# A hybrid recurrent decoder step: the end in three stretches, the merges and the residual's norm on VectorE, the samples' passes spread

## The chip, the cores and the metric

The kernel runs on one core of one Trainium2 chip. The metric is the device time of one execution in microseconds (us); smaller is better. The engines are TensorE (PE, with its weight loads as PEld), VectorE (DVE), ScalarE (ACT), GpSimd (POOL) and the DMA queues that SyncE (SP) and ScalarE issue.

## The reference

One layer is computed for 544 tokens that share all weights: a prompt of 512 and eight samples of 4 tokens. Model width 1024, feed-forward width 4096, all in float32.

```python
proj = x @ w_in + b_in                    # gates, queries, keys, values of three branches
o, s = _gated_linear_scan(q, k, v, g, s0)     # GLA and HGRN2; mLSTM has a scan of its own
gates = sigmoid(mg).reshape(..., 3, D_MODEL)
merged = (gates[:, :, 0] * (h_gla @ w_up_gla)
          + gates[:, :, 1] * (h_ml @ w_up_ml)
          + gates[:, :, 2] * (h_hg @ w_up_hg))
x = _layernorm(DN_ALPHA * x + merged @ w_out, ln1_g, ln1_b)
hid = square(relu(x @ w_ff_up))
x = _layernorm(DN_ALPHA * x + hid @ w_ff_down, ln2_g, ln2_b)
```

The outputs are x and the branches' new states, for the prompt and for the samples.

## The kernel before

**Layout and precision.** Activations are kept transposed: the channels lie on 128 partitions (KD = 8 column tiles for the width of 1024), and the 544 tokens are the free dimension, in two halves of HT = 272. Each operand of a large product is split into a rounded part (`h`) and the rest (`l`) in the type fp32r, and each product is three matmuls per block of 128: wh·xh, wh·xl, wl·xh. For each of them both halves of the tokens are streamed, each into its half of a PSUM tile of the pool `psg` (two buffers). `mm` (L145) writes these matmuls, and nearly all of TensorE's work is its line L158. `gemm` (L163) gets a weight tile ready by `wload` (L133): SP's queue loads `raw`, ScalarE copies it to `wh` (L141), VectorE subtracts to get `wl` (L142), two buffers each. A 128x1024 weight tile has 48 matmuls.

**Stages, in order of time.** The input projections; the mLSTM branch in chunks of 128 tokens; the GLA branch and the HGRN2 branch (`gated`, names with `hg`), whose matmuls run between those of the projections; the merges; the output projection and the first norm's sums; two feed-forward blocks (`blk`) of 16 up tiles (`wff1`, k = x1h, x1l) and 8 down tiles (`wff2`, k = hidh, hidl); the last norm and the stores of y.

- *Samples' passes* (L503): in `gated`, the state of each of eight samples (`Ss`) is multiplied with 2x4 columns of the queries, for two pairs of heads; 16 matmuls in a group, one group in GLA (96 weight columns), one in HGRN2 (64). A matmul in plain f32 shows as two records in the trace.
- *Merges* (class `Merge`): a tile of gates is multiplied with a product from PSUM (L871, VectorE), and in the second and third branch it is added to `merged` (L875, POOL); in the third, the sum is split to `mh` and `ml`, the operands of the output projection.
- *Up tiles*: the norm isn't applied to x1 ahead of the product. It is folded in behind it: VectorE adds `ne` times a column sum (L1029, this reads PSUM), multiplies by `rstd` (L1030), ScalarE takes relu and square, and the result is split. `ne` and `rstd` come from `ln_sums` (L978: TensorE sums `a1`, `a2` over the partitions with a matrix of ones) and `ln_end` (L985, L988).
- *Residual's norm* (L1042 to L1044): the normed x1 itself is wanted only by the down tiles of the first block. From the third up tile on, one column tile beside each up tile: POOL adds `ne`, POOL multiplies by `rstd`, ScalarE applies scale and bias.
- *The end* (L1069 to L1102): the last two column tiles of the second block (`last`, i = 0 and 1) aren't done in full width one after the other. Their four weight tiles (`lh`, `ll`) stay in SBUF; for the first half of the tokens both column tiles are computed (96 matmuls), then the norm's sums of this half are closed, and its norm, in 8 column tiles (VectorE L1092, L1096; ScalarE L1100) and four stores (L1102), lies beside the matmuls of the second half. What follows the second half's last matmul is the tail of the kernel.

**What sets the order.** Each engine takes its instructions in one fixed order. That order is made by a scheduler that is given the program in the order of the code; it plays the engines forward with costs of its own, and of the instructions that are ready in that play it takes the one of highest priority, by default the earlier in the code. `tc.high_priority(OFF)` lifts an instruction far ahead of that; with a negative argument it is put as many places later. DMA transfers of weights stand in SP's queue in their order.

Of the kernel before, what the change touches and what calls it, by code (L numbers as in the profile page):

```python
# [42 lines left out]
def build(tc, I, O):  # L43
    nc = tc.nc
    with ExitStack() as ctx:
# [83 lines left out]
        def vcol(c):  # L129
            return vec[:, c:c + 1]  # L130
# [11 lines left out]
                nc.vector.tensor_tensor(out=l[:, 0:n], in0=raw[:, 0:n], in1=h[:, 0:n].bitcast(F32), op=ALU.subtract)  # L142
            return h, l

        def mm(ps, units, ah, al, ext=0, halves_=(0, 1), between=None):  # L145


            nk = sum(u[2] for u in units)
            k = 0
            for u, (h, l, n) in enumerate(units):  # L150
                if u and between:
                    between()
                for i in range(n):
                    wh, wl = h[:, i * 128:(i + 1) * 128], l[:, i * 128:(i + 1) * 128]
                    for s, (w, a) in enumerate(((wh, ah), (wh, al), (wl, ah))):
                        for hf in halves_:
                            w_ = HT + (ext if hf else 0)
                            nc.tensor.matmul(  # L158
                                ps[:, hf, 0:w_], w, a(k)[:, hf * HT:hf * HT + w_],
                                start=(k == 0 and s == 0), stop=(k == nk - 1 and s == 2))  # L160
                    k += 1

# [184 lines left out]
        def gated(q, k, b, sc, dv, vtok, sname, nt, gate):  # L347
# [142 lines left out]
            def sample():  # L490
                at, P, qx, k3 = (st[2][n] for n in ("at", "P", "qx", "k3"))
                oT = psr.tile([128, 512], F32, tag="r", name="oTs")
                for h in range(4):
                    nc.tensor.matmul(oT[0:dv, h * 32:(h + 1) * 32], vtok[0:32, 4, h * dv:(h + 1) * dv], at[0:32, h, 0:32],
                                     start=(h == 0), stop=False)
                v3 = stack_v(vtok[0:32, 4, 0:d4], d4)
                nb = 512 // dv // 4 * 4
                yield
                for p in range(2):
                    Ss = t1.tile([128, 8, 97], F32, tag="Ss", name="Ss")  # L500
                    nc.scalar.dma_start(out=Ss[:, :, 0:dv], in_=I[sname][p])
                    for n in range(8):
                        nc.tensor.matmul(  # L503
                            oT[0:dv, p * 64:(p + 1) * 64].rearrange("p (a b) -> p a b", a=2)[:, :, 4 * n:4 * n + 4],
                            Ss[:, n, 0:dv], qx[:, p, n], start=False, stop=(p == 1 and n == 7))
                    yield
                    vxs = [spread_v(v3[:, (2 * p + e) * dv:(2 * p + e + 1) * dv], dv, True) for e in range(2)]
                    for n0 in range(0, 8, nb):
                        kvs = psr.tile([128, 512], F32, tag="r", name="kvs")
                        for e in range(2):  # L510
                            nc.tensor.matmul(kvs[:, 0:nb * dv], k3[:, p, e, :], vxs[e][:, n0 * dv:(n0 + nb) * dv], start=(e == 0), stop=(e == 1))
                        for n in range(n0, n0 + nb):
                            nc.vector.scalar_tensor_tensor(
                                Ss[:, n, 0:dv], Ss[:, n, 0:dv], P[:, p, 4 * n + 3:4 * n + 4],
                                kvs[:, (n - n0) * dv:(n - n0 + 1) * dv], ALU.mult, ALU.add)
                    nc.scalar.dma_start(out=O[sname + "_s"][p], in_=Ss[:, :, 0:dv])
                    yield
# [324 lines left out]
        class Merge:  # L842
# [23 lines left out]
            def products(self, m0, n=4):  # L866
                for m in range(m0, m0 + n):
# [3 lines left out]
                        nc.vector.tensor_tensor(out=halves(merged[:, m, :] if self.first else g), in0=ps, in1=halves(g), op=ALU.mult)  # L871
                    if self.first:
                        continue
                    eng = nc.gpsimd
                    eng.tensor_tensor(out=merged[:, m, :], in0=merged[:, m, :], in1=g, op=ALU.add)  # L875
# [98 lines left out]
        def ln_sums(hf, stop=True):  # L974
            s = slice(hf * HT, (hf + 1) * HT)
            ps = [psr.tile([128, 512], F32, tag="r", name=n) for n in ("m1", "m2")]
            for p, a in zip(ps, (a1, a2)):
                nc.tensor.matmul(p[:, 0:HT], onesn, a[:, s], start=True, stop=stop)  # L978
            return ps

        def ln_end(hf, sums, more=()):
            s = slice(hf * HT, (hf + 1) * HT)
            p1, p2 = sums
            for p, a in zip(sums, more):
                nc.tensor.matmul(p[:, 0:HT], onesn, a, start=False, stop=True)  # L985
            e2 = rstd[:, s]
            nc.scalar.activation(out=e2, in_=p1[:, 0:HT], func=AF.Square)
            nc.vector.tensor_tensor(out=e2, in0=p2[:, 0:HT], in1=e2, op=ALU.subtract)  # L988
            nc.scalar.activation(out=ne[:, s], in_=p1[:, 0:HT], func=AF.Copy, scale=-1.0)
# [22 lines left out]
            nc.vector.scalar_tensor_tensor(halves(x1[:, m, :]), halves(xr), ALPHA, ps, ALU.mult, ALU.add)  # L1012
            ln_tile(x1, m, slice(0, T), put_x1)
        for hf in range(2):
            ln_end(hf, ln_sums(hf))
        mps.close()


# [1 line left out]
        for blk in range(2):  # L1020
            hid = []
            deep = [hl3("hdh", "hh"), hl3("hdl", "hl")] + [w6.tile([128, 3 * T], F32R, tag="w6", name="hdw").rearrange("p (a b) -> p a b", a=3) for i in range(2)]
            for m in range(16):
# [13 lines left out]
                    l = fp.tile([128, T], F32R, tag=f"hidl{m}", name="hidl")  # L1037
                split(h, l, r_)
                hid.append((h, l))
                if blk == 0 and 2 <= m < 2 + KD:  # L1040
                    y = x1[:, m - 2, :]
                    nc.gpsimd.tensor_tensor(out=y, in0=y, in1=ne, op=ALU.add)  # L1042
                    nc.gpsimd.tensor_tensor(out=y, in0=y, in1=rstd, op=ALU.mult)  # L1043
                    nc.scalar.activation(out=y, in_=y, func=AF.Identity, scale=vcol(V_L1G + m - 2), bias=vcol(V_L1B + m - 2))  # L1044
# [21 lines left out]
        for i in range(2):  # L1066
            y = x1[:, KD - 2 + i, :]
            nc.vector.tensor_tensor(out=y, in0=y, in1=cm, op=ALU.subtract)
        pss = [psg.tile([128, 2, 512], F32, tag="g", name="g") for i in range(2)]  # L1069
        def last(i, hf, sl, between=None):  # L1070
            y = x1[:, KD - 2 + i, sl]
            mm(pss[i], units[2 * i:2 * i + 2], hh_, hl_, halves_=(hf,), between=between)
            sq = ftile("sq")
            with tc.high_priority(OFF):
                nc.vector.tensor_tensor(out=y, in0=y, in1=pss[i][:, hf, 0:HT], op=ALU.add)
                nc.scalar.activation(out=sq[:, sl], in_=y, func=AF.Square)
            return y, sq[:, sl]

        for hf in range(2):
            sl = slice(hf * HT, (hf + 1) * HT)  # L1080
            y, sq = last(0, hf, sl)
            with tc.high_priority(OFF):
                nc.vector.tensor_tensor(out=a1[:, sl], in0=a1[:, sl], in1=y, op=ALU.add)
                nc.vector.tensor_tensor(out=a2[:, sl], in0=a2[:, sl], in1=sq, op=ALU.add)
            ends = []
            more = last(1, hf, sl, lambda: ends.append(ln_sums(hf, False)))
            with tc.high_priority(OFF):
                ln_end(hf, ends[0], more)
            for m in range(KD):
                y = x1[:, m, sl]  # L1090
                eng = nc.gpsimd if m in ADDP else nc.vector
                eng.tensor_tensor(out=y, in0=y, in1=ne[:, sl], op=ALU.add)  # L1092
            for m in range(KD):
                y = x1[:, m, sl]
                eng = nc.gpsimd if m in MULP else nc.vector
                eng.tensor_tensor(out=y, in0=y, in1=rstd[:, sl], op=ALU.mult)  # L1096
                if m in AFFD:
                    nc.vector.tensor_scalar(y, y, vcol(V_L2G + m), vcol(V_L2B + m), ALU.mult, ALU.add)
                else:
                    nc.scalar.activation(out=y, in_=y, func=AF.Identity, scale=vcol(V_L2G + m), bias=vcol(V_L2B + m))  # L1100
# [124 lines left out]
```

## Time and profile before

| | us |
|---|---|
| three runs | 940.23, 935.35, 938.45 |
| their median | 938.45 |
| the profiled execution | 940.08 |
| its span in the trace | 938.2 |
| TensorE busy in it | 916.5 (98%) |
| VectorE busy | 556.8 (59%) |
| ScalarE busy | 437.4 (47%) |
| POOL busy | 101.1 (11%) |
| mean granted TensorE clock | 0.991 |

The trace counts from the start of the span. "L158" is line 158 of the kernel before; in the changed kernel lines lie a few further down (L158 is L162 there, L1029 is L1034, L1096 is L1102). A row of a timeline has the start, the time from the first to the last of the instructions that it groups, engine, line and operation, out<-in, the shape, their count, and in brackets the idle time ahead with what ended it. A row of a matmul has the active rows*columns of the weights ahead of the streamed shape. Rows by stretches have busy time (with the number of instructions) of PE, PEld, DVE, ACT and POOL, and then the granted clock (1.00 is full), the share of the DMA engines and the GB/s.

### The profile page before, as it was taken

The page shows a single profiled execution, that of the slowest core. Times are in us where ns is not written, and L with a number is a line of the kernel's source. Part 1 is how long each engine was busy: PE and PEld are TensorE (multiplying, and loading weights), DVE is VectorE, ACT ScalarE, POOL GpSimd, SP SyncE. Part 2 cuts the span into 40 slices and gives each one's busy share as a digit, 9 for nine tenths or more (in the row PEclk, how much of TensorE's full clock was granted, in tenths as well). Part 3 has the DMA queues.
Part 4 walks back from the last instruction along what each step waited for, and adds up shares of the span by engine and source line. Part 5 has one row for each costly group of instructions (what it writes and reads, how often), then busy time and mean ns, then how long its engine had stood idle before and what let it go on. Part 6 is the DMA issues. An engine that isn't in the chain of part 4 may idle for free.

```text
span 938.2 us, 17454 instructions
## 1 busy us (share of the span) xinstructions
PE 916.5 (98%) x7279; PEld 900.4 (96%) x7279; DVE 556.8 (59%) x959; ACT 437.4 (47%) x824; POOL 101.1 (11%) x92
## 2 busy tenths in 40 slices
PE   9999999999999999999999998999999999999995
PEld 7998999999999998999999998999999999999994
DVE  5885568858788577874458656553222355545435
ACT  4296132875636674634444356552111354442315
POOL 0301231001001003131110092000000000000000
PEclk9999999989999999999999999999999999999998
DMA  7311132114132213132234322222222222222302
GB/s 264 121 69 68 59 113 83 40 46 135 41 113 73 76 29 110 35 98 87 68 113 146 106 68 90 92 90 89 86 79 86 90 91 91 91 89 77 105 23 96
DMA packets 37598, 82.73 MB, mean 88 GB/s; under 512 B 12708, under 2 KB 18340, under 8 KB 37520
## 3 DMA queue, kind: packets, MB, share of 16 engines
q1 hardware_dynamic: 25072, 73.28, 24.0%
q10 hardware_dynamic: 12384, 8.33, 3.1%
q8 instruction: 57, 0.93, 0.4%
q14 instruction: 21, 0.17, 0.1%
q0 software_dynamic: 64, 0.02, 0.0%
HBM read 76.51 MB, written 5.09 MB: 87 GB/s over the span
## 4 chain that ended last, share of the span: by engine, by line
PE 86%; DVE 5%; POOL 3%; ACT 3%; DMA 1%; issue 1%; POOLq 0%; ACTq 0%; DVEq 0%
PE g L158 73%; PE lv L406 3%; PE g L83 2%; DVE wl L142 2%; POOL merged L1043 1%; ACT wh L141 1%; POOL merged L1042 1%; DMA Cs<-in_mC 1%; PE o L463 1%; POOL cvo L586 1%; PE oTs L503 1%; PE oTm L763 1%; PE qkp L676 0%; DMA fw<-in_wfirst 0%; PE oT L282 0%
## 5 line engine op out<-in xcount | busy, mean ns | idle before, releaser
L142 DVE TENSOR_TENSOR wl<-raw,wh 128x1024 fp32r<-128x1024 f32 (+2 forms) x139 | 158.1, 1138 | 144.0 <-ACT wh L141 142.2
L141 ACT ACTIVATE wh<-raw 128x1024 fp32r<-128x1024 f32 (+2 forms) x139 | 133.2, 958 | 231.0 <-PE g L158 196.4
L158 PE MATMUL g<-xh,wl 128*128 128x272 f32 x752 | 161.9, 294 | 2.9 <-DVE wl L142 2.9
L158 PE MATMUL g<-xl,wh 128*128 128x272 f32 x752 | 160.3, 292 | 0.0
L158 PE MATMUL g<-xh,wh 128*128 128x272 f32 x752 | 159.8, 292 | 0.0
L158 PEld LDWEIGHTS g<-xh,wl 128*128 128x128 f32 x752 | 120.1, 190 | 5.1 <-DVE wl L142 4.7
L158 PEld LDWEIGHTS g<-xl,wh 128*128 128x128 f32 x752 | 120.0, 190 | 0.8 <-issue 0.5
L158 PEld LDWEIGHTS g<-xh,wh 128*128 128x128 f32 x752 | 119.7, 190 | 0.9 <-issue 0.2
L158 PE MATMUL g<-x1h,wh 128*128 128x272 f32 (+1 forms) x512 | 106.5, 289 | 3.2 <-DVE relu L1029 3.2
L158 PE MATMUL g<-x1l,wh 128*128 128x272 f32 (+1 forms) x512 | 106.7, 289 | 0.0
L158 PE MATMUL g<-x1h,wl 128*128 128x272 f32 (+1 forms) x512 | 106.0, 288 | 0.0
L158 PEld LDWEIGHTS g<-x1h,wh 128*128 128x128 f32 x512 | 80.8, 189 | 3.6 <-DVE relu L1029 3.6
L158 PEld LDWEIGHTS g<-x1l,wh 128*128 128x128 f32 x512 | 81.5, 190 | 0.1
L158 PEld LDWEIGHTS g<-x1h,wl 128*128 128x128 f32 x512 | 81.0, 188 | 0.0
L1031 ACT ACTIVATE relu<-relu,gw 128x544 f32<-128x544 f32 x32 | 24.0, 750 | 77.2 <-DVE relu L1030 77.2
L158 PE MATMUL g<-hidh,wh 128*128 128x272 f32 x280 | 58.1, 288 | 0.0
L158 PE MATMUL g<-hidl,wh 128*128 128x272 f32 x280 | 58.1, 289 | 0.0
L158 PE MATMUL g<-hidh,wl 128*128 128x272 f32 x280 | 57.8, 288 | 0.0
L158 PEld LDWEIGHTS g<-hidl,wh 128*128 128x128 f32 x280 | 44.0, 188 | 0.0
L158 PEld LDWEIGHTS g<-hidh,wl 128*128 128x128 f32 x280 | 43.9, 188 | 0.0
L158 PEld LDWEIGHTS g<-hidh,wh 128*128 128x128 f32 x280 | 43.8, 188 | 0.0
L410 DVE COPY_PREDICATED at<-lmask,lv 128x512 f32<-128x512 int32 (+1 forms) x32 | 26.2, 819 | 22.2 <-PE lv L406 18.2
(399 smaller groups left out, 1695.4 us busy)
## 6 DMA issues: line engine op xcount, KB each, us to landing
raw<-in_wff SPq DMA_DIRECT2D x64, 512.0 KB, 3.5
raw<-in_win SPq DMA_DIRECT2D x47, 512.0 KB, 3.3
xr<-in_xT SPq DMA_DIRECT2D x16, 272.0 KB, 3.3
raw<-in_wout SPq DMA_DIRECT2D x8, 512.0 KB, 3.9
out_yT<-merged SPq DMA_DIRECT2D x8, 272.0 KB, 2.2
fw<-in_wfirst ACTq DMA_DIRECT2D x8, 256.0 KB, 5.2
raw<-in_wup_ml SPq DMA_DIRECT2D x8, 192.0 KB, 2.3
raw<-in_wup_gla SPq DMA_DIRECT2D x8, 192.0 KB, 2.3
```

Of the source, the lines that this page charges most:

```text
L83: nc.tensor.matmul(first_ps[i][hf], w[:, i * 128:(i + 1) * 128], a[:, k, hf * HT:(hf + 1) * HT], start=(k == 0 and n == 0), stop=(k == KD ...
L141: nc.scalar.activation(out=h[:, 0:n], in_=raw[:, 0:n], func=AF.Copy)
L142: nc.vector.tensor_tensor(out=l[:, 0:n], in0=raw[:, 0:n], in1=h[:, 0:n].bitcast(F32), op=ALU.subtract)
L158: nc.tensor.matmul(ps[:, hf, 0:w_], w, a(k)[:, hf * HT:hf * HT + w_], start=(k == 0 and s == 0), stop=(k == nk - 1 and s == 2))
L406: nc.tensor.matmul(lv[0:R, o:o + 2 * H].rearrange("p (a b) -> p a b", a=2), Kv[:, p, c * R:(c + 1) * R], Q[:, p, :, c * H:(c + 1) * H], st ...
L410: nc.vector.copy_predicated(atv.rearrange("p h (n m) -> p h n m", m=2 * m)[:, :, :, m:2 * m], lmask[0:R, li, 0:H].rearrange("p (n m) -> p ...
L463: nc.tensor.matmul(o[:, h * dv:(h + 1) * dv], at[:, c * 4 + h, :], vtok[:, cc, h * dv:(h + 1) * dv], start=(h == 0), stop=(cc == 0 and h = ...
L503: nc.tensor.matmul(oT[0:dv, p * 64:(p + 1) * 64].rearrange("p (a b) -> p a b", a=2)[:, :, 4 * n:4 * n + 4], Ss[:, n, 0:dv], qx[:, p, n], s ...
L586: nc.gpsimd.tensor_copy(cvo[:, :, 0, :], xcp[:, :, 512:515])
L763: nc.tensor.matmul(oT[0:97, h * 32 + 4 * n:h * 32 + 4 * n + 4], Cs[:, n, :], qF[h][:, 4 * n:4 * n + 4], start=False, stop=(h == 3 and n == 7))
L1031: nc.scalar.activation(out=r_, in_=r_, func=AF.Relu, bias=gw[:, 1:2])
L1042: nc.gpsimd.tensor_tensor(out=y, in0=y, in1=ne, op=ALU.add)
```

## The change

1. **The end in three stretches.** `LAST = (0, 272, 408, 544)`: the last two column tiles are finished for 272, then 136, then 136 tokens. `mm_to` takes a list of (output, first token) in place of a choice of halves, and each stretch and column tile takes its own PSUM tile. `ln_sums` and `ln_end` take a slice.
2. **Merges.** The additions to `merged` go from POOL to VectorE: 16 instructions.
3. **The residual's norm.** The additions of `ne` and the multiplications by `rstd` go from POOL to VectorE, 16 instructions; column tile m // 2 gets its addition beside an even up tile m, and its multiplication and ScalarE's pass beside the odd one that follows. It starts with up tile 0 and not 2.
4. **The samples' passes.** Each of the matmuls of L503 gets a priority 380 + 4n places later (`BEHIND`), n being the sample.

The choices of engine `ADDP`, `MULP`, `AFFD`, all empty before, are taken out, which changes nothing.

```diff
+BEHIND = 380
+LAST = (0, 272, 408, 544)
...
-                        for hf in halves_:
-                            w_ = HT + (ext if hf else 0)
+                        for o, t0 in outs:
                             nc.tensor.matmul(
-                                ps[:, hf, 0:w_], w, a(k)[:, hf * HT:hf * HT + w_],
+                                o, w, a(k)[:, t0:t0 + o.shape[-1]],
...
                     for n in range(8):
-                        nc.tensor.matmul(
+                        with tc.high_priority(-(BEHIND + 4 * n)):
+                            nc.tensor.matmul(
...
-                    eng = nc.gpsimd
-                    eng.tensor_tensor(out=merged[:, m, :], in0=merged[:, m, :], in1=g, op=ALU.add)
+                    nc.vector.tensor_tensor(out=merged[:, m, :], in0=merged[:, m, :], in1=g, op=ALU.add)
...
-                if blk == 0 and 2 <= m < 2 + KD:
-                    y = x1[:, m - 2, :]
-                    nc.gpsimd.tensor_tensor(out=y, in0=y, in1=ne, op=ALU.add)
-                    nc.gpsimd.tensor_tensor(out=y, in0=y, in1=rstd, op=ALU.mult)
-                    nc.scalar.activation(out=y, in_=y, func=AF.Identity, scale=vcol(V_L1G + m - 2), bias=vcol(V_L1B + m - 2))
+                if blk == 0:
+                    y = x1[:, m // 2, :]
+                    if m % 2 == 0:
+                        nc.vector.tensor_tensor(out=y, in0=y, in1=ne, op=ALU.add)
+                    else:
+                        nc.vector.tensor_tensor(out=y, in0=y, in1=rstd, op=ALU.mult)
+                        nc.scalar.activation(out=y, in_=y, func=AF.Identity, scale=vcol(V_L1G + m // 2), bias=vcol(V_L1B + m // 2))
...
-        pss = [psg.tile([128, 2, 512], F32, tag="g", name="g") for i in range(2)]
-        def last(i, hf, sl, between=None):
+        def last(i, sl, between=None):
             y = x1[:, KD - 2 + i, sl]
-            mm(pss[i], units[2 * i:2 * i + 2], hh_, hl_, halves_=(hf,), between=between)
+            n = sl.stop - sl.start
+            ps = psg.tile([128, 2, 512], F32, tag="g", name="g")[:, 0, 0:n]
+            mm_to([(ps, sl.start)], units[2 * i:2 * i + 2], hh_, hl_, between)
...
-        for hf in range(2):
-            sl = slice(hf * HT, (hf + 1) * HT)
-            y, sq = last(0, hf, sl)
+        for sl in (slice(a, b) for a, b in zip(LAST, LAST[1:])):
+            y, sq = last(0, sl)
...
-            more = last(1, hf, sl, lambda: ends.append(ln_sums(hf, False)))
+            more = last(1, sl, lambda: ends.append(ln_sums(sl, False)))
```

**What it does to the engines' orders.** At the start of the feed-forward part VectorE's order, before and after (the second ends of `rstd`, then the residual's norm, the first weight splits and the first relus; the x8 is a group of eight alike in a row):

```order
L988 TENSOR_TENSOR rstd<-m_6316,rstd 128x272
L988 TENSOR_TENSOR rstd<-m_6325,rstd 128x272
L142 TENSOR_TENSOR wl<-raw,wh 128x1024
L1029 SCALAR_TENSOR_TENSOR relu<-ne,gw,g 128x544
L1030 TENSOR_TENSOR relu<-relu,rstd 128x544
L142 TENSOR_TENSOR wl<-raw,wh 128x1024
L1029 SCALAR_TENSOR_TENSOR relu<-ne,gw,g 128x544
L180 TENSOR_TENSOR hdw<-relu,hdh 128x544
```

```order
L992 TENSOR_TENSOR rstd<-m_6316,rstd 128x272
L992 TENSOR_TENSOR rstd<-m_6325,rstd 128x272
L1049 TENSOR_TENSOR merged<-merged,ne 128x544 x8
L143 TENSOR_TENSOR wl<-raw,wh 128x1024
L1034 SCALAR_TENSOR_TENSOR relu<-ne,gw,g 128x544
L1051 TENSOR_TENSOR merged<-merged,rstd 128x544 x8
L143 TENSOR_TENSOR wl<-raw,wh 128x1024
L1034 SCALAR_TENSOR_TENSOR relu<-ne,gw,g 128x544
L1035 TENSOR_TENSOR relu<-relu,rstd 128x544 x2
```

All eight additions stand ahead of the first relu, and all eight multiplications ahead of the second; the code has one of them beside each up tile, but they are ready early and come by their own priority.

TensorE's order in GLA, where the first group of samples' passes (L503, L509 after) stands among the projections' matmuls (g) and those of a chunk's attention (lv):

```order
L503 MATMUL oTs<-qx,Ss 96x2x4 x16
L158 MATMUL g<-xl,wh 128x272
L158 MATMUL g<-xh,wl 128x272 x2
L158 MATMUL g<-xh,wh 128x272 x2
L158 MATMUL g<-xl,wh 128x272 x2
L158 MATMUL g<-xh,wl 128x272 x2
L406 MATMUL lv<-qe_2105,ke_2103 128x128 x4
```

```order
L509 MATMUL oTs<-qx,Ss 96x2x4 x9
L162 MATMUL g<-xl,wh 128x272
L162 MATMUL g<-xh,wl 128x272
L509 MATMUL oTs<-qx,Ss 96x2x4
L162 MATMUL g<-xh,wl 128x272
L162 MATMUL g<-xh,wh 128x272 x2
L162 MATMUL g<-xl,wh 128x272
L509 MATMUL oTs<-qx,Ss 96x2x4
```

Nine of the sixteen stay together, and the other seven stand alone, each behind three or four full matmuls. Of the second group, 8, 2 and 6 together before, two stay together and 14 stand alone.

VectorE's order in the merges of the second branch, near 370 us of the trace, where the last chunks of HGRN2 still run (S, at, dsb are a state, attention weights, decays):

```order
L871 TENSOR_TENSOR gb<-g,gb 128x544
L142 TENSOR_TENSOR wl<-raw,wh 128x384
L368 COPY dsb<-dps 128x8
L410 COPY_PREDICATED at<-lmask,lv 128x8x64
L477 COPY S<-kvp 64x64 x3
L871 TENSOR_TENSOR gb<-g,gb 128x544
L477 COPY S<-kvp 64x64
L142 TENSOR_TENSOR wl<-raw,wh 128x1024
```

```order
L877 TENSOR_TENSOR gb<-g,gb 128x544
L372 COPY dsb<-dps 128x8
L143 TENSOR_TENSOR wl<-raw,wh 128x1024
L880 TENSOR_TENSOR merged<-merged,gb 128x544
L877 TENSOR_TENSOR gb<-g,gb 128x544
L880 TENSOR_TENSOR merged<-merged,gb 128x544
L414 COPY_PREDICATED at<-lmask,lv 128x8x64
L481 COPY S<-kvp 64x64 x4
L143 TENSOR_TENSOR wl<-raw,wh 128x1024
```

The additions (L880) follow their multiplications (L877), and a 128x1024 split now stands ahead of them and of the copies of `S`. In SP's queue the eight last stores of 272 tokens become four of 272 and eight of 136.

More of the change, by code (lines that the diff above doesn't have):

```diff
@@ L27 @@
 OFF = 1000000
+BEHIND = 380
 NF = 4
 NWARM = 10
-ADDP, MULP, AFFD = (), (), ()
+LAST = (0, 272, 408, 544)
 LEVELS = (64, 32, 16, 8, 4, 2, 1)
@@ L143, in wload, with mm, mm_to @@
             return h, l
-        def mm(ps, units, ah, al, ext=0, halves_=(0, 1), between=None):
+        def mm(ps, units, ah, al, ext=0):
+            mm_to([(ps[:, hf, 0:HT + (ext if hf else 0)], hf * HT) for hf in range(2)], units, ah, al)
+        def mm_to(outs, units, ah, al, between=None):
             nk = sum(u[2] for u in units)
@@ L502, in sample @@
                     for n in range(8):
-                        nc.tensor.matmul(
-                            oT[0:dv, p * 64:(p + 1) * 64].rearrange("p (a b) -> p a b", a=2)[:, :, 4 * n:4 * n + 4],
-                            Ss[:, n, 0:dv], qx[:, p, n], start=False, stop=(p == 1 and n == 7))
+                        with tc.high_priority(-(BEHIND + 4 * n)):
+                            nc.tensor.matmul(
+                                oT[0:dv, p * 64:(p + 1) * 64].rearrange("p (a b) -> p a b", a=2)[:, :, 4 * n:4 * n + 4],
+                                Ss[:, n, 0:dv], qx[:, p, n], start=False, stop=(p == 1 and n == 7))
                     yield
@@ L972, in ln_tile, with ln_sums, ln_end @@
                 nc.vector.tensor_tensor(out=a2[:, sl], in0=a2[:, sl], in1=sq[:, sl], op=ALU.add)
-        def ln_sums(hf, stop=True):
-            s = slice(hf * HT, (hf + 1) * HT)
-            ps = [psr.tile([128, 512], F32, tag="r", name=n) for n in ("m1", "m2")]
+        def ln_sums(s, stop=True):
+            n = s.stop - s.start
+            ps = [psr.tile([128, 512], F32, tag="r", name=n_)[:, 0:n] for n_ in ("m1", "m2")]
             for p, a in zip(ps, (a1, a2)):
-                nc.tensor.matmul(p[:, 0:HT], onesn, a[:, s], start=True, stop=stop)
+                nc.tensor.matmul(p, onesn, a[:, s], start=True, stop=stop)
             return ps
-        def ln_end(hf, sums, more=()):
-            s = slice(hf * HT, (hf + 1) * HT)
+        def ln_end(s, sums, more=()):
             p1, p2 = sums
             for p, a in zip(sums, more):
-                nc.tensor.matmul(p[:, 0:HT], onesn, a, start=False, stop=True)
+                nc.tensor.matmul(p, onesn, a, start=False, stop=True)
             e2 = rstd[:, s]
-            nc.scalar.activation(out=e2, in_=p1[:, 0:HT], func=AF.Square)
-            nc.vector.tensor_tensor(out=e2, in0=p2[:, 0:HT], in1=e2, op=ALU.subtract)
-            nc.scalar.activation(out=ne[:, s], in_=p1[:, 0:HT], func=AF.Copy, scale=-1.0)
+            nc.scalar.activation(out=e2, in_=p1, func=AF.Square)
+            nc.vector.tensor_tensor(out=e2, in0=p2, in1=e2, op=ALU.subtract)
+            nc.scalar.activation(out=ne[:, s], in_=p1, func=AF.Copy, scale=-1.0)
             nc.scalar.activation(out=e2, in_=e2, func=AF.Ln, bias=epsl)
@@ L1014, in build @@
         for hf in range(2):
-            ln_end(hf, ln_sums(hf))
+            s = slice(hf * HT, (hf + 1) * HT)
+            ln_end(s, ln_sums(s))
         mps.close()
@@ L1068, in build @@
             nc.vector.tensor_tensor(out=y, in0=y, in1=cm, op=ALU.subtract)
-        pss = [psg.tile([128, 2, 512], F32, tag="g", name="g") for i in range(2)]
-        def last(i, hf, sl, between=None):
+        def last(i, sl, between=None):
             y = x1[:, KD - 2 + i, sl]
-            mm(pss[i], units[2 * i:2 * i + 2], hh_, hl_, halves_=(hf,), between=between)
+            n = sl.stop - sl.start
+            ps = psg.tile([128, 2, 512], F32, tag="g", name="g")[:, 0, 0:n]
+            mm_to([(ps, sl.start)], units[2 * i:2 * i + 2], hh_, hl_, between)
             sq = ftile("sq")
             with tc.high_priority(OFF):
-                nc.vector.tensor_tensor(out=y, in0=y, in1=pss[i][:, hf, 0:HT], op=ALU.add)
+                nc.vector.tensor_tensor(out=y, in0=y, in1=ps, op=ALU.add)
                 nc.scalar.activation(out=sq[:, sl], in_=y, func=AF.Square)
             return y, sq[:, sl]
-        for hf in range(2):
-            sl = slice(hf * HT, (hf + 1) * HT)
-            y, sq = last(0, hf, sl)
+        for sl in (slice(a, b) for a, b in zip(LAST, LAST[1:])):
+            y, sq = last(0, sl)
             with tc.high_priority(OFF):
@@ L1085, in build @@
             ends = []
-            more = last(1, hf, sl, lambda: ends.append(ln_sums(hf, False)))
+            more = last(1, sl, lambda: ends.append(ln_sums(sl, False)))
             with tc.high_priority(OFF):
-                ln_end(hf, ends[0], more)
+                ln_end(sl, ends[0], more)
             for m in range(KD):
                 y = x1[:, m, sl]
-                eng = nc.gpsimd if m in ADDP else nc.vector
-                eng.tensor_tensor(out=y, in0=y, in1=ne[:, sl], op=ALU.add)
+                nc.vector.tensor_tensor(out=y, in0=y, in1=ne[:, sl], op=ALU.add)
             for m in range(KD):
                 y = x1[:, m, sl]
[L1095 to L1100, printed above, removed]
+                nc.vector.tensor_tensor(out=y, in0=y, in1=rstd[:, sl], op=ALU.mult)
+                nc.scalar.activation(out=y, in_=y, func=AF.Identity, scale=vcol(V_L2G + m), bias=vcol(V_L2B + m))
                 if m % 2:
```

## The prediction

> **What bounds the kernel now.** I read the page, then the chain of waits, then TensorE's waits, then timelines of single stretches.
>
> ```profile
> PE 916.5 (98%) x7279; PEld 900.4 (96%) x7279; DVE 556.8 (59%) x959; ACT 437.4 (47%) x824; POOL 101.1 (11%) x92
> 843.86 65.25 PE g L158 x520
> PE g L158 <- DVE wl L142: 4.3, 9, 1.7
> PE g L158 <- DVE relu L1029: 3.2, 2, 1.6
> ```
>
> TensorE is busy for 98% of the span, so the time moves only by the matmuls' own time, by the few stops between them, and by what follows the last one. Pitch below means from start to start. Back to back, a 128x272 matmul has a pitch of 65.25 / 520 = 0.1255 us (second line, from the chain). The last two lines (waits: us in all, times, longest) are the stops within the change's reach. The profiled execution took 940.08 us, 1.88 of them outside its span of 938.2, and lies 1.6 above the median of 938.45. I work against 940.08.
>
> **The end, the largest term.** Today two passes over 272 tokens, each 96 matmuls; after, one such pass and two of 136 tokens, each again 96 matmuls with 96 weight loads: 96 matmuls of 272 become 192 of 136. No row shows one of those. These bound it (weight loads grouped by form, the mean ns ahead of the last bar; then timelines: start, us):
>
> ```profile
> L158 PEld LDWEIGHTS g<-xh,wl 128*128 128x128 f32 x752 | 120.1, 190 | 5.1 <-DVE wl L142 4.7
> L365 PEld LDWEIGHTS dps<-small,qk 128*128 128x128 f32 x32 | 3.9, 191 | 0.0
> L695 PEld LDWEIGHTS <-identb 128*128 128x128 bf16 x4 | 0.4, 98 | 0.1
> 224.22 0.81 PE L365 MATMUL dps<-small,qk 128*128 128x2 f32 x6
> 224.89 0.37 PE L158 MATMUL g<-xl,wh 128*128 128x272 f32 x1
> 96.51 0.24 PE L699 MATMUL dp<-rd,ones 36*32 36x128 f32 x1
> 332.52 1.04 PE L503 MATMUL oTs<-qx,Ss 128*64 128x8 f32 x15
> ```
>
> Streaming alone would be half of 0.1255, 0.063. But the dps matmuls stream two columns and are still (224.89 - 224.22) / 6 = 0.112 apart; the oTs ones, with 64 weight columns instead of 128, about (1.04 - 0.20) / 14 = 0.060. So a short matmul waits for its weights, by their columns. Our load (190 ns) is as long as that of dps (191), so I take its 0.112: 192 x 0.112 - 96 x 0.1255 = 21.50 - 12.05 = +9.45. Bounds: 0.063 if the loads hide (+0.05), and 0.1255 if the width saves nothing (+12.05). (Plain f32 matmuls run as two records each. Ours are fp32r, a rounded f32 that runs as one; the last but one line, 128 columns in fp32r, is one record too, so I count one at 136.)
>
> The Trainium skill, page "TensorE: Matmul & The Clock Gate", section "Weight-path perf modes — Fast Weight Load (FWL) and DoubleRow", says that loads of 128 weights are sped up, up to fourfold, unless the type is FP32. The bf16 row (98) agrees with it, the 190 of our type does not. If it held here, the 136-wide passes would cost almost nothing, as in the second rival.
>
> The norm's sums and the tail:
>
> ```profile
> 925.16 1.08 PE L978 MATMUL m<-a,onesn 128*128 128x272 f32 x4
> 927.26 0.44 DVE L988 TENSOR_TENSOR rstd<-m,rstd 128x272 f32<-128x272 f32 x1 [1.46 <-PE m L985]
> 927.62 2.89 DVE L1092 TENSOR_TENSOR merged<-merged,ne 128x272 f32<-128x272 f32 x8
> 930.43 2.90 DVE L1096 TENSOR_TENSOR merged<-merged,rstd 128x272 f32<-128x272 f32 x8
> 930.90 4.14 ACT L1100 ACTIVATE merged<-merged,vec 128x272 f32<-128x272 f32 x8 [2.18 <-DVE merged L1096]
> 497.11 1.35 DVE L965 TENSOR_TENSOR merged<-merged,cm 128x544 f32<-128x544 f32 x2
> 562.98 0.83 ACT L1044 ACTIVATE merged<-merged,vec 128x544 f32<-128x544 f32 x1
> 563.71 0.15 ACT L1027 ACTIVATE gw<-g 128x2 f32<-128x2 f32 x1
> ```
>
> A sum is two records of about 0.23 at 272, so 0.23 in all at 136. Five more of these (four of the middle stretch, one of the last) stand in the stream: +1.15. The tail is 938.2 - 925.16 = 13.04. VectorE's pitch is 2.81 / 8 = 0.35 at 272 (from L1092 to L1096) and about 0.63 at 544 (L965), so 0.21 at 136; ScalarE's 0.51 at 272 and 0.73 at 544, so 0.40. At 136 the eight additions of ne save 8 x 0.14 = 1.1, ScalarE's eight passes 0.9, the sums and squares up to 927.26 about 0.8, the shorter single steps 0.4; the last store is left as it is (12 stores for 8, alone in SP's queue). Tail -3.2, between -2 and -5. The middle stretch's norm (16 VectorE steps of 0.21, 8 ScalarE steps of 0.40) lies beside 10.7 us of matmuls. The end: 9.45 + 1.15 - 3.2 = **+7.4**.
>
> **The samples' passes.**
>
> ```profile
> 185.95 1.97 PE L503 MATMUL oTs<-qx,Ss 128*96 128x8 f32 x22
> 184.35:187.76 3.41, 3.41 (x38) 3.37 (x38) 3.26 (x7) 3.38 (x10) 0.00 (x0) 1.00 0.10 36
> 187.76:194.59 6.83, 6.83 (x35) 6.83 (x35) 4.04 (x9) 5.58 (x16) 0.20 (x1) 0.50 0.11 31
> 129.62 0.28 PE L158 MATMUL g<-xl,wh 128*128 128x272 f32 x1
> 129.74 0.25 PE L731 MATMUL cp<-cols,lastsel 128*96 128x4 f32 x2
> 130.06 0.42 PE L158 MATMUL g<-xh,wl 128*128 128x272 f32 x2
> ```
>
> From 185.95 stand 32 records of 8 columns in a row, and right after the stretch that they fill the granted clock falls to 0.50 for 6.83 us (third line; the clock is the third number from its end). TensorE was never idle there; it streamed little. After, nine pairs stay together (18 x 0.085 = 1.5 us) and seven stand alone among full matmuls. The second group of 16 pairs, in three blocks today, shows no fall. So I take the fall as gone: half of 6.83 less the 0.2 that stay lost, -3.2. Single pairs cost 130.06 - 129.62 - 2 x 0.1255 = 0.19 each (cp) against 2 x 0.085 in a block, fewer where 64 columns are loaded: +0.5 for 21 of them.
>
> The same page, section "Part 1: The HAM clock gate (the "warmup" mystery)", has the clock halved after an idle window of about 3.4 us. Here it fell without idling, so the row goes further than the rule; by the rule alone, neither this fall nor one in the first rival would be.
>
> **Merges on VectorE.** 16 POOL instructions become 16 of 0.63 on VectorE: 10 us of an engine that is 59% busy. POOL's queue holds nothing else there, so nothing is queued behind them on the old side; on the new side, splits of weight tiles and evacuations are. Where these are early, the cover is the 6 us of a tile's 48 matmuls. At two places before the norm VectorE is waited for today, and the third begins the next part:
>
> ```profile
> 370.25 1.35 POOL L875 TENSOR_TENSOR merged<-merged,gb 128x544 f32<-128x544 f32 x1 [3.49 <-DVE gb L871]
> 370.40 2.28 DVE L142 TENSOR_TENSOR wl<-raw,wh 128x1024 fp32r<-128x1024 f32 x1
> 372.74 0.52 PE L158 MATMUL g<-xh,wl 128*128 128x272 f32 x2 [1.74 <-DVE wl L142]
> 480.76 3.52 DVE L142 TENSOR_TENSOR wl<-raw,wh 128x1024 fp32r<-128x1024 f32 x2 [0.24 <-ACT wh L141]
> 483.19 0.39 PE L158 MATMUL g<-mh,wl 128*128 128x272 f32 x1 [1.44 <-DVE wl L142]
> 539.96 0.44 DVE L988 TENSOR_TENSOR rstd<-m,rstd 128x272 f32<-128x272 f32 x1 [0.47 <-PE m L978]
> 541.51 1.55 DVE L142 TENSOR_TENSOR wl<-raw,wh 128x1024 fp32r<-128x1024 f32 x1 [1.10 <-ACT wh L141]
> 542.98 0.77 DVE L1029 SCALAR_TENSOR_TENSOR relu<-ne,gw,g 128x544 f32<-128x544 f32 x1
> 545.22 0.41 PE L158 MATMUL g<-x1h,wh 128*128 128x272 f32 x2
> ```
>
> At 370 the split of a weight tile takes 2.28 while POOL adds, and stands behind copies of a state; of the pair at 480 the first ends where TensorE starts again (483.19, 2.4 after the pair's start), so the second takes the other 1.1. POOL's addition thus costs the split some 1.1 here, and after the change it stands ahead of the copies. I take -1.6 of the stop of 1.74. At 480 the first of two splits is slowed in the same way; the addition (0.63) now stands ahead of it: -0.8. Bounds of the two together: -3.2 if both stops go, +1.3 if the additions only delay the splits.
>
> **Residual's norm on VectorE.** What moves: all eight additions of ne stand ahead of the split and the relu of the first up-projection tile, and all eight multiplications ahead of those of the second. VectorE is free at 540.4: eight additions to 545.7, split to 546.8, relu to 547.6 (today 543.75). The third tile, which starts at 545.22, needs the PSUM buffer that this relu frees: it starts at 547.6, a new stop of 2.4. Then eight multiplications to 552.6, split and relu to 554.5, where the fourth tile could start at 553.7: 0.9. After that, ScalarE's eight affine passes (0.73 each, now behind VectorE and no longer behind POOL) end at 554.1 and delay the fifth tile's split to 555.2 on ScalarE, 557.0 on VectorE; the relu for it ends at 560.6, just as the fourth tile does. So nothing later waits. Against these 3.3 stand today's two stops for relu:
>
> ```profile
> 565.08 0.39 PE L158 MATMUL g<-x1h,wh 128*128 128x272 f32 x1 [1.57 <-DVE relu L1029]
> 563.23:566.64 3.41, 1.84 (x15) 1.63 (x14) 3.38 (x4) 3.19 (x6) 3.41 (x3) 1.00 0.37 108
> 570.05:573.46 3.41, 1.81 (x14) 1.59 (x13) 2.44 (x3) 2.19 (x4) 0.00 (x0) 1.00 0.18 18
> 85.36:88.77 3.41, 3.25 (x23) 2.60 (x22) 1.59 (x3) 1.52 (x3) 2.29 (x5) 1.00 0.00 0
> 88.77:92.19 3.42, 3.42 (x17) 3.42 (x17) 2.66 (x4) 2.53 (x5) 0.00 (x0) 0.50 0.00 0
> ```
>
> They are 3.2 by the waits, 3.5 with the pitch lost around them: **-0.2**, with bounds of -3.5 (no new stop) and +3 (the new ones beside the old).
>
> **The sum.** 7.4 - 3.2 + 0.5 - 1.6 - 0.8 - 0.2 = +2.1, so 942.2; rounded, 942.0 us, 0.4% above the median shown. About 0.5% (4.7 us) is what a measurement of this kernel can tell from no change.
>
> **Rivals.** First, slower: the new stop of 2.4 us at 545 halves the clock. The last four rows above are stretches of 3.41, the step in which this clock changes: with today's stops in them TensorE was still busy for 1.84 and 1.81, and the clock held; behind 85.36, where matmuls of 32 rows stood, it fell though TensorE was busy. A stop of 2.4 leaves 1.0 of 3.41, less than any stretch in which it held, if the stop lies within one. Price: up to half of 3.41 for one window or of 6.83 for two, +1.7 to +3.4: 943.9 to 945.6. The point from which it decides is about 1.7 to 2 us of stop inside one such stretch. Chance 0.28.
>
> Second, faster: the loads of the 136-wide matmuls hide, 0.063 each: 942.2 - 9.4 = 932.8. For it: at 272 the load of 190 ns is hidden in a pitch of 125. Against: dps. Chance 0.10.
>
> Third, the spreading does not do what it is for: the clock falls after the nine pairs too: +3.2, 945.4. For it: with the block of lv behind them, nine pairs still leave a window at about a third. Chance 0.15.
>
> Forecast as summed: 0.47. The 136-wide pitch at 0.125 moves it by 2.6 and other new stops of the changed order by 1 or 2, so part of the forecast also ends above 943.1. Same 0.52, slower 0.38, faster 0.10. The range 936 to 946.5 leaves out most of the second rival and the sum of both slower ones.
>
> **What would show it.** Right: a pitch near 0.112 for the 128x136 matmuls; 9 to 10 us from the last matmul to the end; a clock of 1.00 around 188; no wl wait at 370; a stop of about 2.4 for relu L1034 in front of the third up-projection tile and none of 1.6 later. Wrong: a pitch near 0.063 or above 0.13, a clock of 0.50 behind 545, or TensorE waiting in the reordered stretch between 190 and 430, where I assume no new stop.

## The result, and the profile after

The changed kernel is slower: 947.24 us (median of 6 runs, 944.43 to 950.13) against 938.27 (6 runs, 934.92 to 940.23). The ratio is 1.0107, with a 95% interval of 1.0086 to 1.0129. 942.0 with a range up to 946.5 was forecast, so the direction of the sum (+2.1) was right, and its size a quarter of the 9.0.

The profiled execution took 946.15 us, 1.1 below its median, as that of before was 1.8 above its own. So the two traces are only 5.9 us apart, and the rest of the 9.0 comes from which execution of each kernel was profiled (where the clock fell is a part of that, see below).

First lines from the page, the chain and TensorE's waits of the changed kernel:

```profile
PE 927.3 (98%) x7383; PEld 909.2 (96%) x7383; DVE 570.1 (60%) x1012; ACT 440.8 (47%) x838; POOL 46.5 (5%) x60
841.78 65.25 PE g L162 x520
PE g L162 <- DVE relu L1034: 2.2, 1, 2.2
PE g L162 <- DVE wl L143: 1.9, 7, 0.7
PE lv L410 <- DVE qe L402: 0.7, 1, 0.7
```

TensorE is again busy for 98% of a longer span. The stretch of 520 matmuls is the same 65.25 and begins 2.08 earlier than before (843.86). Of these 2.08, 1.87 come from the start, which the change doesn't touch; up to there its gains and losses nearly cancel (-0.2), and the loss of this trace lies behind. The stop for wl of 1.74 is gone, the two for relu have become one of 2.2, and there is a new wait of lv.

Stage by stage, from the start of ScalarE's copy of the same weight tile in both traces (us):

| stretch before | after minus before | what differs |
|---|---|---|
| 0 to 186.66 | -1.87 | nothing of the change: the start (three executions of the changed kernel end this stretch between 184.66 and 185.98) |
| 186.66 to 229.11 | -2.30 | GLA's passes spread; clock 1.00, not 0.50; wait of lv |
| 229.11 to 328.57 | +0.13 | |
| 328.57 to 362.41 | +3.63 | HGRN2's passes spread |
| 362.41 to 387.37 | -2.19 | merges |
| 387.37 to 540.42 | -0.07 | merges; the stop at 481 is 0.7 shorter, one at 430 is new |
| 540.42 to 609.33 | +0.58 | residual's norm; a fall of the clock |
| 609.33 to 875.16 | +0.01 | |
| 875.16 to the end | +8.04 | three stretches |

The end (the first row, from the chain, is matmuls of 136 alone; the others are from the timeline):

```profile
914.26 9.00 PE g L162 x81
933.64 0.44 PE L983 MATMUL m<-a,onesn 128*128 128x136 f32 x2
935.36 1.76 DVE L1099 TENSOR_TENSOR merged<-merged,ne 128x136 f32<-128x136 f32 x8
937.37 3.24 ACT L1103 ACTIVATE merged<-merged,vec 128x136 f32<-128x136 f32 x8 [1.14 <-DVE merged L1102]
```

9.00 / 81 = 0.111 is the pitch of a 136-wide matmul. From the end of the last product, where the sum in the second row starts, to the end of the span it is 944.1 - 933.64 = 10.5, against 938.2 - 925.16 = 13.0 before. (After the change the first of the two sums stands ahead of that, at 931.84.)

### The profile page after: what moved, and what is told of

It reads as the page before. It is cut to its first block, busy times and chain, and to the rows that moved or that the text cites. A ratio compares the mean times of both kernels' runs of the same rounds, so it can differ in the third digit from the quotient of the medians.

```text
span 944.1 us, 17687 instructions
## 1 busy us (share of the span) xinstructions
PE 927.3 (98%) x7383; PEld 909.2 (96%) x7383; DVE 570.1 (60%) x1012; ACT 440.8 (47%) x838; POOL 46.5 (5%) x60
## 4 chain that ended last, share of the span: by engine, by line
PE 88%; DVE 5%; ACT 3%; DMA 2%; issue 1%; POOL 1%; ACTq 0%; SPq 0%; DVEq 0%
PE g L162 77%; PE lv L410 3%; DVE wl L143 1%; DMA xr<-in_xT 1%; ACT wh L142 1%; PE o L467 1%; POOL cvo L592 1%; PE oTs L509 1%; PE oTm L769 1%; DMA Cs<-in_mC 1%; PE qkp L682 0%; PE oT L286 0%; PE o L470 0%; DVE merged L1049 0%; DMA raw<-in_win 0%
## 5 line engine op out<-in xcount | busy, mean ns | idle before, releaser
L143 DVE TENSOR_TENSOR wl<-raw,wh 128x1024 fp32r<-128x1024 f32 (+2 forms) x139 | 155.6, 1120 | 135.1 <-ACT wh L142 133.1
L219 DVE TENSOR_SCALAR gb<-g,vec 128x544 f32<-128x544 f32 x24 | 18.8, 783 | 31.5 <-PE g L162 31.3
```

The costliest lines, as they stand in the source:

```text
L219: nc.vector.tensor_scalar(out, ps, vcol(col), XMIN, ALU.add, ALU.max)
```

## The experiments

Each kernel is timed beside the kernel before (938.38, 21 runs, in the first group; 938.12, 17 runs, in the second; 940.12, one run, beside the two repeats). "Clock lost" is span times (1 - mean granted clock) of a run; in the twelve traces 3.0 to 4.4 of it lie behind the last matmul, where TensorE has nothing left to do. The clock is on record to three digits, so a single run's loss is good to about 0.5.

**The end alone taken back.**

```diff
-LAST = (0, 272, 408, 544)
+LAST = (0, 272, 544)
```

> The changed kernel with the end in two stretches of 272 again; the rest of the change stays. Theory A (the third stretch costs what its weight loads cost: 192 matmuls of 0.112 for 96 of 0.126, +9.4, +1 for sums, -2.7 of tail): 8 us less than the changed kernel's 947.2, so 939.2, and the last matmul 10.7 earlier. Rival B (the middle stretch is cheap, and most of the 9 us come from the other parts): at most 3 less, 944 or more.

938.71 (12 runs), a ratio of 1.0009 (0.9995 to 1.0024) to before: 8.5 less than the changed kernel. The stretch from tile 875 to the end is 8.05 shorter. Theory A holds: the third stretch alone is the size of the whole loss. All the rest of the change, gains and losses together, came to nothing.

**HGRN2's passes together again, GLA's still spread.**

```diff
-with tc.high_priority(-(BEHIND + 4 * n)):
+with tc.high_priority(-(BEHIND + 4 * n) if dv == 96 else 0):
```

> The changed kernel, but HGRN2's samples' passes (64 weight columns) keep their own priority and stand together as before; GLA's (96 columns) stay spread. Theory A (a pair of 64 columns alone among full matmuls costs 0.40 of TensorE and 0.12 in a block, 14 of them): 3.6 less, 943.6, and the stretch from 324.5 to 362.0 is 33.9 long in place of 37.5. Rival B (that stretch is longer for other reasons, the merges' additions or the waits of lv): it stays above 36.5 and the time above 946.

943.84 (6 runs), ratio 1.0054 (1.0034 to 1.0074): 3.4 less than the changed kernel. The stretch by windows (busy time of PE, PEld, DVE, ACT and POOL with counts, clock, DMA share, GB/s), of before, changed, and this kernel:

```profile
328.57:362.41 33.84, 33.84 (x286) 32.58 (x285) 25.13 (x55) 22.70 (x58) 3.58 (x3) 1.00 0.17 49
324.53:362.00 37.47, 37.47 (x286) 34.19 (x285) 25.82 (x55) 22.02 (x56) 2.56 (x2) 1.00 0.19 54
322.73:356.59 33.86, 33.86 (x286) 32.61 (x285) 25.14 (x55) 22.70 (x59) 2.88 (x2) 1.00 0.17 49
```

The same 286 matmuls, at a full clock and without an idle TensorE, take 37.47 when the passes are spread and 33.86 when they are together. So it is the passes' spreading, and no wait.

**HGRN2's passes spread, but with 96 weight columns.**

```diff
-oT[0:dv, ...], Ss[:, n, 0:dv], qx[:, p, n]
+oT[0:96, ...], Ss[:, n, 0:96], qx[:, p, n]    # columns 64 to 95 are zero
...
```

The four matmuls that open this sum (values times attention) are widened to 96 columns with it.

> The changed kernel, but HGRN2's samples' passes load 96 weight columns in place of 64 (the 32 more are zeros, their results are not read), still spread one by one. Theory A (the width of 64 is what makes a single pair dear; at 96, as in GLA, it costs 0.19): 14 x (0.40 - 0.19) = 2.9 less, 944.3, although more weights are loaded. Rival B (a pair alone in HGRN2 costs 0.40 for its place in the stream, whatever its width): no change or 14 x 0.05 more, 947 to 948.

945.11 (8 runs), ratio 1.0055 (1.0036 to 1.0074): 2.1 less in the median, 3.0 less in the stretch itself. Timelines of a pair alone, first in the changed kernel, then here, and the stretch here:

```profile
341.63 0.28 PE L162 MATMUL g<-xh,wh 128*128 128x272 f32 x1
341.84 0.28 PE L509 MATMUL oTs<-qx,Ss 128*64 128x8 f32 x2
342.05 0.39 PE L162 MATMUL g<-xh,wh 128*128 128x272 f32 x1
342.28 0.41 PE L162 MATMUL g<-xl,wh 128*128 128x272 f32 x2
...
342.29 0.29 PE L162 MATMUL g<-xl,wh 128*128 128x272 f32 x1
342.41 0.26 PE L511 MATMUL oTs<-qx,Ss 128*96 128x8 f32 x2
342.52 0.37 PE L162 MATMUL g<-xl,wh 128*128 128x272 f32 x1
342.73 0.42 PE L162 MATMUL g<-xh,wl 128*128 128x272 f32 x2
...
324.37:358.82 34.45, 34.45 (x286) 33.67 (x285) 24.97 (x54) 21.68 (x56) 2.77 (x2) 1.00 0.20 56
```

With 64 columns, two full matmuls and the pair take 342.28 - 341.63 = 0.65, so the pair costs 0.65 - 2 x 0.126 = 0.40. With 96 it is 342.73 - 342.29 = 0.44, and the pair costs 0.19, although half as many weights again are loaded. Fourteen times the difference is 2.9, the 3.0 of the stretch, so the four other matmuls that were widened matter little. In the narrow case the pair starts 0.21 behind the matmul ahead of it, not 0.12, and the matmul behind the pair is late as well. So the width of 64 is what is dear, and only next to full-width work: in a block the prediction's row has about 0.06 for a record, 0.12 for a pair.

**The residual's norm tied to its up tiles.**

```diff
+one = fp.tile([128, 1], F32, tag="one", name="one", bufs=3)
+nc.scalar.activation(out=one, in_=gw[:, 0:1], func=AF.Copy, scale=0.0, bias=1.0)
-nc.vector.tensor_tensor(out=y, in0=y, in1=ne, op=ALU.add)
+nc.vector.scalar_tensor_tensor(y, y, one, ne, ALU.mult, ALU.add)   # rstd likewise
```

> The changed kernel, but each step of the residual's norm on VectorE takes a factor of 1 that ScalarE makes from the up tile beside it, so that it can't run ahead of that tile: one step per tile, 16 of 0.77. Theory A (eight additions in a row make the stop of 2.5 in front of the third up tile, and the stop halves TensorE's clock for one or two windows of 3.4): both go, 2.5 + 1.7 to 3.4 = 4.2 to 5.9 less, 941.3 to 943.0, clock 1.00 around 545. Rival B (the clock falls somewhere there anyway, since relu is waited for twice in any case): 2.5 less at most, 944.7, with a clock of 0.50 in some window between 540 and 575.

944.75 (8 runs), ratio 1.0057 (1.0034 to 1.0080): 2.5 less than the changed kernel. No wait for relu is left. VectorE's timeline, changed kernel and then this one:

```profile
542.98 1.22 DVE L143 TENSOR_TENSOR wl<-raw,wh 128x1024 fp32r<-128x1024 f32 x1
544.12 0.78 DVE L1034 SCALAR_TENSOR_TENSOR relu<-ne,gw,g 128x544 f32<-128x544 f32 x1
544.81 5.17 DVE L1051 TENSOR_TENSOR merged<-merged,rstd 128x544 f32<-128x544 f32 x8
...
542.05 1.22 DVE L143 TENSOR_TENSOR wl<-raw,wh 128x1024 fp32r<-128x1024 f32 x1 [1.10 <-ACT wh L142]
543.19 0.77 DVE L1034 SCALAR_TENSOR_TENSOR relu<-ne,gw,g 128x544 f32<-128x544 f32 x1
543.88 0.78 DVE L1051 SCALAR_TENSOR_TENSOR merged<-merged,one,ne 128x544 f32<-128x544 f32 x1
```

The stage from 540 to 609 is 3.69 shorter than before here and 0.58 longer in the changed kernel, 4.3 between them, and the clock is 1.00 throughout it, as theory A has it. The median moved by only 2.5, which is the number of B without its sign (a clock of 0.50 between 540 and 575). In this execution the clock fell near 187, in the changed kernel's it did not, and its runs lost 7.0 us of clock on the mean, no less than the changed kernel's 6.9: on the whole program one fall gone didn't make the loss smaller. That asked for more traces of one kernel.

**The changed kernel, profiled twice more.**

> The changed kernel as it is, one more profiled execution, to see which windows of 3.41 have a clock of 0.50. Theory A (a window's boundary lies at random to the program; a fall comes only where one window holds most of the stop near 543, or little but short matmuls near 185): the program's times between two places agree with the first execution's to 0.2 us except where the clock fell, and falls need not lie at the same places. Rival B (a fall belongs to its place): 0.50 behind the stop near 545 again, and none near 187.

> The same once more, with the same two readings: by theory A the stop near 543 is followed by a clock of 0.50 only where a window holds it wholly, with TensorE busy for about 1.2 of 3.4; where it is split over two windows (2.8 and 1.8, as with the end in two stretches) there is none.

950.27 and 948.28 us, one run each. The windows of 3.41 with the stop in them, and the one behind, from the changed kernel's first, second and third execution, and a second stop of the third:

```profile
541.62:545.04 3.42, 1.18 (x10) 0.96 (x8) 3.42 (x6) 1.12 (x2) 0.00 (x0) 1.00 0.00 0
545.04:548.46 3.42, 3.42 (x15) 3.42 (x16) 3.42 (x6) 2.90 (x4) 0.00 (x0) 0.50 0.46 153
...
545.54:548.95 3.41, 1.49 (x12) 1.27 (x11) 3.41 (x5) 1.12 (x2) 0.00 (x0) 1.00 0.00 0
548.95:552.36 3.41, 3.09 (x13) 3.09 (x14) 3.41 (x7) 2.48 (x4) 0.00 (x0) 0.50 0.49 154
...
544.20:547.61 3.41, 1.54 (x13) 1.32 (x11) 3.41 (x5) 1.12 (x2) 0.00 (x0) 1.00 0.00 0
547.61:551.03 3.42, 3.05 (x24) 3.06 (x25) 3.42 (x7) 2.44 (x4) 0.00 (x0) 1.00 0.45 153
554.89 0.52 PE L162 MATMUL g<-x1h,wh 128*128 128x272 f32 x2 [0.60 <-DVE relu L1034]
```

The stop is the same in all three, but the window's boundary isn't at the same place of the program. With TensorE busy for 1.18 and 1.49 of 3.41 the next window has half the clock; with 1.54 it hasn't, nor with 1.72 in the kernel with 96 columns, 1.99 in that with two stretches (541.79 to 545.20, the clock's own step there; the 2.8 and 1.8 expected above were of other windows), or the 1.81 and 1.84 of before. The third execution also had the second stop, 0.60 of idling and 0.9 from start to start, which is missing where the slow window came first: the stage from 540 to 609 is 0.8 to 0.9 longer with the fall than without, not 1.7. Near 187:

```profile
183.23:186.65 3.42, 3.42 (x36) 3.42 (x36) 3.28 (x6) 3.37 (x10) 0.00 (x0) 1.00 0.00 0
186.65:190.06 3.41, 3.41 (x31) 3.41 (x30) 1.83 (x4) 3.41 (x10) 0.00 (x0) 1.00 0.22 62
...
182.39:185.80 3.41, 3.41 (x38) 3.37 (x37) 3.26 (x7) 3.39 (x10) 0.00 (x0) 1.00 0.07 24
185.80:192.63 6.83, 6.83 (x36) 6.83 (x34) 2.49 (x5) 4.83 (x14) 0.00 (x0) 0.50 0.10 31
```

The first two rows are the first execution, the others the third. A window that lies 0.7 earlier in the program makes the clock fall for 6.83. So A holds, save that the executions also differ by up to 2.0 in their first 45 us. Of seven executions with nine pairs together, over all kernels, four had this fall; of three with all sixteen together, three; of two with three together at first, none. Counted from the start of ScalarE's copy at 184.79 (the tile that the table starts its second row with), the seven windows began 2.74, 2.54, 2.27 and 2.26 ahead where it fell, and 2.84, 1.56 and 1.46 ahead where it held. So the fall goes with the place of the window, and these traces alone can't tell sixteen or three from nine: their windows began 2.39, 2.31 and 2.13 ahead (sixteen) and 1.94 and 1.11 (three).

**The merges alone.** The kernel before, with one edit:

```diff
-                    eng = nc.gpsimd
+                    eng = nc.vector
```

> The kernel before with one part of the change alone, the 16 additions of the merges on VectorE. Theory A (the split of a weight tile is slowed while POOL adds; without that the stop of 1.7 at 370 goes and the one at 481 shrinks by 0.7, as in the changed kernel): 2.2 to 2.7 less than before, 935.7, and no wait of TensorE for wl over 1 us but one of 1.0. Rival B (the gain comes from what else moved there, and the additions only hold up VectorE's queue): 938 or more, with a wait for wl at 370.

935.14 (12 runs), ratio 0.9972 (0.9955 to 0.9989): 3.0 less than before. TensorE's waits:

```profile
PE g L158 <- DVE relu L1029: 3.1, 2, 1.6
PE g L158 <- DVE wl L142: 1.9, 7, 0.7
```

The stop of 1.74 for wl is gone and the other is at 0.7, as with the whole change. VectorE's splits at the two places, here:

```profile
366.90 1.23 DVE L142 TENSOR_TENSOR wl<-raw,wh 128x1024 fp32r<-128x1024 f32 x1
477.69 2.35 DVE L142 TENSOR_TENSOR wl<-raw,wh 128x1024 fp32r<-128x1024 f32 x2
```

They took 2.28 and 3.52 while POOL added, so 1.05 and 1.17 of the gain are the splits' own time, and A holds for that. What makes up the rest at 370 isn't shown; VectorE's order differs there too (a masked copy of attention weights that stood ahead of this split stands behind it).

**The parts that pay, together.**

```diff
+LAST = (0, 272, 544)       # two stretches
+with tc.high_priority(0):  # all samples' passes in their own order
+...                        # merges on VectorE, norm tied as above
```

> The changed kernel without the parts that cost: two stretches of 272, all samples' passes together as before, the residual's norm tied to the up tiles on VectorE; the merges stay on VectorE. From the stages of the earlier runs: merges -2.2, norm -3.7 (both stops for relu gone), the rest as before: 932.4. In the traces of the kernels with 32 short records in a row the clock falls for two windows there; theory A: it does so here in every run, share of clock lost as before (7.8 us by span times 1 - clock).

930.73 (6 runs), ratio 0.9932 (0.9910 to 0.9953): 7.4 less than before, and 1.7 us faster than expected. The mean loss of clock is 7.4, as the block of sixteen leads one to expect, and the trace has the fall at 185.93. But A's "every run" doesn't hold: one run lost only 5.6, less than the 3.6 behind the last matmul and the 3.4 of such a fall together.

**And GLA's passes spread further.**

```diff
-BEHIND + 4 * n
+BEHIND + 24 * n    # GLA's only
```

> As b1_together, but GLA's samples' passes (96 columns) are spread further than in the change: three together at most at first, five at the end. Theory A (the clock falls behind a block because the block fills most of a window of 3.4; nine pairs with lv's matmuls ahead were still enough in some runs, by where the window lies): with three the fall near 187 is gone in every run, 3.4 less, 929.0, and clock lost 4.4. Rival B (a fall is a matter of chance and comes elsewhere instead): 932 as b1, clock lost still 7 or more.

930.44 (6 runs), ratio 0.9923 (0.9903 to 0.9943). The clock lost went to 5.4 (least 3.7), 2.0 less and not 3.4: near 187 there is no fall, but this execution had one of 3.41 at 112 (eight of the other eleven traces have one near 87, and this one hasn't). Neither theory's numbers came. And the 2.0 didn't reach the time. TensorE's waits here, and then in b1:

```profile
PE g L162 <- DVE wl L143: 2.3, 8, 0.7
PE g L162 <- DVE merged L877: 1.5, 1, 1.5
...
PE g L162 <- DVE wl L143: 1.9, 7, 0.7
PE g L162 <- DVE merged L877: 0.3, 1, 0.3
```

A merge is waited for 1.2 longer; that the later passes hold up VectorE's work in front of it is likely and not shown. The wait of lv isn't there. Whether the spreading is worth anything stays open; the two kernels can't be told apart.

**An uneven end.**

```diff
-LAST = (0, 272, 544)
+LAST = (0, 300, 544)
```

> As b2_gla_spread, but the end in two stretches of 300 and 244. Theory A (a matmul takes the longer of its weight load, 0.112, and 0.46 ns a column; 244 columns are just at the load): 96 x (0.138 + 0.112 - 0.251) = 0 for the matmuls, and a tail shorter by 28 of 272 columns, 0.4 less, 928.6, pitch at 244 of 0.112. Rival B (under 256 columns a matmul takes longer than its load): pitch over 0.12 and a time above b2_gla_spread.

930.13 (6 runs), ratio 0.9926 (0.9905 to 0.9947), the same as b2 within what can be told. Two rows of its timeline, nine matmuls apart:

```profile
913.19 0.28 PE L162 MATMUL g<-hidh,ll 128*128 128x244 f32 x1
914.21 0.28 PE L162 MATMUL g<-hidh,ll 128*128 128x244 f32 x1
```

(914.21 - 913.19) / 9 = 0.113: 244 columns are still at the price of the weight load, like 136 (0.111), and B's 0.12 is out. So A holds for the pitch. The 0.4 of tail is below what the times can show.

## Why the prediction was wrong, point by point

The sum was +2.1, measured are +9.0 between the medians and +6.1 between the two profiled executions (946.15 - 940.08). Without the start, which isn't the change's, the two traces are 7.8 apart, 5.7 more than the sum: 3.1 of it in HGRN2's single pairs, 0.9 in GLA's stretch, 0.8 in the norm's, 0.6 in the end, and 0.3 in the rest.

- **The end, +7.4: right, a little small.** The measure is +8.0 by the stage and +8.5 by the runs. The pitch was 0.112 as taken from dps: a matmul as wide as 136 waits for its weights, and the second rival (0.063) is out. The tail fell by 2.5 and not 3.2: VectorE's and ScalarE's passes came out about as worked out, but up to the first addition of ne 0.7 was saved (927.62 - 925.16 = 2.46, now 935.36 - 933.64 = 1.72) where 0.8 and a part of 0.4 stood, and from ScalarE's last pass to the end of the span it is 944.1 - 937.37 - 3.24 = 3.5, before 938.2 - 930.90 - 4.14 = 3.2.
- **Single pairs, +0.5: the step that failed.** I took 0.19 from cp, which loads 96 columns, and wrote "fewer where 64 columns are loaded". The price goes the other way: 0.40 at 64. 14 x (0.40 - 0.12) = 3.9, and 3.6 was measured over the stretch. For GLA's 96 columns the 0.19 was right. The sum was also too low by its own rows: with 0.19 for a single pair and 0.12 for one in a block, the fourteen come to 1.0 and not to a part of 0.5.
- **The fall at 187, -3.2: mis-sized.** The third rival (0.15) was nearer than the forecast: with nine pairs together the fall came in four of seven traces. On the mean the runs lost 6.9 us of clock after, and 7.8 and 7.3 in the two groups of before, a gain of 0.4 to 0.9. By an estimate, a run that lost less than 6 had no fall near 187 (3.0 or more are lost at the end, 3.4 by the fall). With sixteen together these are 8 of 56 runs, with nine 10 of 42, with three at first 9 of 12: nine were still enough in many runs. GLA's spreading also brought the wait of lv (0.7 by the waits, 0.9 from start to start), which is in all seven of these traces, in none of the three with sixteen together, and not in the two where it is spread further.
- **Merges, -2.4: right.** -3.0 alone by the runs, with an interval that holds -2.4 (-4.2 to -1.0), and the splits are faster by the 1.1 that was named.
- **The residual's norm, -0.2: right without the clock.** With two stretches, where the clock held, the stage is 0.3 shorter than before; where it fell, 0.58 longer. So the first rival (0.28), that the stop halves the clock, came true in two of three traces of the changed kernel (three of six with the others that have the stop), at 0.8 to 0.9 each and not 1.7 to 3.4. The stops of 2.4 and 0.9 in front of the third and fourth up tile are there (2.2 and 0.6 by the waits). But I put today's two stops against it as if both had to be paid: tied to the tiles, neither is, which is worth 3.7.
- **The base.** One profiled execution was taken as the kernel. Which falls it had, and how long its start took, differ from execution to execution: runs of before lie between 933.4 and 940.5.

By the Trainium skill, page "TensorE: Matmul & The Clock Gate", section "Part 1: The HAM clock gate (the "warmup" mystery)", the window is 3.413 us long and free-running. The traces agree: in the second execution the fall behind the stop begins 548.95 - 187.13 = 361.82 = 106 x 3.413 after the one near 187, and each execution has its windows at other places of the program. It puts the halving behind an idle window; the rows here show less to be enough: 1.49 of 3.41 busy, and near 187 a window without any idling. In the prediction I read that rule as against a fall; its other half, that the window runs freely, was the part that mattered.

The Trainium skill, page "TensorEngine Tiling (Array Packing)", sections "Key Properties" and "When to Use Tiling", has column tiling, another mode of the array, for weights of up to 64 columns, and says that a change of mode drains TensorE. The two timelines would fit that (0.40 for a pair of 64, 0.19 for one of 96), but no run here shows in which mode these matmuls ran. Why 64 columns are dear stays open; that they are is shown.

## What to carry to other kernels

Halve a pass only as far as its weight loads are hidden: at 0.112 for the load and 0.1255 / 272 = 0.46 ns a column, about 244 columns are the edge here, and below it taking columns off saves nothing. Don't scatter narrow matmuls among wide ones; keep them in a block, or, if they must be scattered, pad them: 96 columns were cheaper here than 64. When an engine gets work from another, give each piece a dependence on the step beside which it is meant to stand: this scheduler found it ready and put all of it first, which the order shows ahead of any run.

## What the runs showed of the hardware that was not expected

- Two records of 64 weight columns between matmuls of 128 cost 0.40 us, of 96 columns 0.19, and in a block of their own kind 0.12 (64) or 0.17 (96).
- The clock's windows of 3.41 lie at other places of the program in each execution. A window with a stop in which TensorE was busy for 1.49 was followed by half the clock, one with 1.54 not; but busy time alone doesn't decide, since near 187 it fell behind 3.41 of 3.41. Where the clock falls goes with how long a run takes (runs of the kernel before lie up to 7 us apart): in the first group the 15 runs that lost 8.4 us of clock took 938.07 to 940.5, the six that lost 6.5 or less 934.93 to 936.56.
- 244 columns take 0.113 and 136 columns 0.111 a matmul: under the weight load's time the width makes next to no difference.
